# Sliding windows by DMA alone: the software ring's rows in 63 small DMAs over the run, let go by SyncE's

## The chip, the cores and the metric

One Trainium2 chip, one of its cores. The metric is the device time of one execution in microseconds (us), the median over runs of the same kernel. A core has 16 DMA engines, which move the data, and several instruction engines, which issue the DMAs. Three of them do so here: SyncE (SP in the profile), ScalarE (ACT) and GpSimd (POOL). Each has a ring of DMA work of its own on all 16 DMA engines. SP's is queue q1 and ACT's q10, both hardware_dynamic, and POOL's is q0, software_dynamic. I call q0 the software ring.

## What is computed

```python
batch, length, dim = (32, 4096, 256)      # float32
window_size, stride = 64, 32
n_windows = (length - window_size) // stride + 1        # 127
for i in range(n_windows):
    start = i * stride
    result[:, i] = x[:, start:start + window_size].copy()
```

It is a pure copy. A batch row of x has 128 blocks of 32 x 256 floats (32 KB each). Window w is blocks w and w + 1, 64 KB in a row, in x as in the output. So each block is written twice, but for the first and the last of a batch: 32 x 127 x 64 KB = 266.3 MB of output.

## The kernel before

The 32 batches are divided in two sets (L151 to L153).

**Staged** batches, 12 of them, go through SBUF on ACT's ring (class Staging). A load (L40) brings the 128 blocks of a batch, 4 MB, into one of six tiles xb; the stores (L49) then write it twice, once as the first half and once as the second half of the windows, in DMAs of 4 MB or 2 MB. Their pieces are 16 KB (IN and OUT, L9). `run` (L121) loads six batches, stores them, loads six more as their tiles come free, and stores those. The last two batches are stored by `store_pair` (L102), which waits once, near the end of the run, until four of its 2 MB stores have landed (semaphore `spilt`).

**Direct** batches, 20 of them, go from x to the output without SBUF. A DMA of SP (`windows`, L29, called by `blocks`, L166) takes one half (32 KB) of each of 16 windows: 512 KB in 16 pieces of 32 KB (DIRECT, L9). 16 x 7 = 112 of a batch's 127 windows go so, in 14 DMAs (`halves`, L174), 280 DMAs in all. 22 of these (`spoilt`, L175) lie next to a staged batch and come last, each after a wait for that batch's stores.

The other 15 windows of each direct batch, windows 48 to 62, are whole rows of 64 KB and go by POOL's ring (`remainder`, L170): one DMA of 15 rows for each of 19 batches; those of the last batch go in one DMA of 11 rows and four DMAs of two half rows. That makes 24 DMAs, 19.66 MB. `piece` is the largest run that one descriptor moves. It is 32 KB, and 16 KB for the 15 rows of the batches with index 0, 1, 2 and 6 and for the half rows.

All of this stands in one critical section (L178): ACT runs Staging, POOL issues its 24 DMAs one after the other without waiting and then drains (L189), and SP issues its 280. SP issues the first of them (L191), then waits for the semaphore `back` (L192), which the DMA of 15 rows of the batch with index 16 of 20 raises when it has landed, and then issues the rest (L193). At the end SP waits for all counts (L200).

The outermost count of an SP DMA's shape is 16 windows; of a POOL DMA's it is the number of rows.

Of the kernel before, what the change touches and what calls it, by code (L numbers as in the profile page):

```python
# [8 lines left out]
DIRECT, IN, OUT = 32768, 16384, 16384  # L9
# [124 lines left out]
@with_exitstack  # L134
def kernel(
    ctx: ExitStack,
    tc: tile.TileContext,
    x: bass.AP,
    window_size: bass.AP,
    stride: bass.AP,  # L140
    out: bass.AP,
):
    nc = tc.nc
    W, S = int(window_size), int(stride)
    B, L, D = x.shape
    n_win = (L - W) // S + 1
    assert out.shape == (B, n_win, W, D)
    c = Copier(x, out, B, L, D, W, S, n_win)


    staged = [1, 4, 7, 10, 13, 16, 19, 22, 24, 26, B - 3, B - 2]  # L151
    place = {b: g for g, b in enumerate(staged)}
    direct = [b for b in range(B) if b not in staged]  # L153
    pool = ctx.enter_context(tc.tile_pool(name="xb", bufs=1))
    st = Staging(c, tc, pool, x.dtype, staged, 6)
    ring_d, ring_s, ring_r = nc.sync, nc.scalar, nc.gpsimd
    done = tc.alloc_semaphore("done")
    rest = tc.alloc_semaphore("rest")
    back = tc.alloc_semaphore("back")
    total = {done: 0, rest: 0, back: 0}  # L160

    def count(dma, sem):
        dma.then_inc(sem, 16)
        total[sem] += 16

    def blocks(part):  # L166
        for b, w, half in part:
            count(c.windows(ring_d, b, w, 16, half), done)

    def remainder(i, b, w, n, half=None, piece=DIRECT):  # L170
        count(c.windows(ring_r, b, w, n, half, piece), back if i == len(direct) - 4 and n == 15 else rest)

    first, last = 48, B - 1
    halves = [(b, w + (15 if w >= first else 0), half) for b in direct for w in range(0, 112, 16) for half in (0, 1)]  # L174
    spoilt = {(b + d, 0 if d > 0 else c.nw - 16, 0 if d > 0 else 1): g for b, g in place.items() for d in (1, -1) if b + d in direct}  # L175
    halves = [h for h in halves if h not in spoilt]
    spoilt = sorted(spoilt, key=spoilt.get)
    with tc.tile_critical():  # L178
        st.run(ring_s)

        pairs = iter([(first + d, half) for d in (0, 2) for half in (0, 1)])
        for i, b in enumerate(direct[:-1]):
            if i in (12, 15, 17, 18):
                w, half = next(pairs)
                remainder(i, last, w, 2, half, DIRECT // 2)
            if i == len(direct) - 2:
                remainder(i, last, first + 4, 11)
            remainder(i, b, first, 15, piece=DIRECT // 2 if i in (0, 1, 2, 6) else DIRECT)
        ring_r.drain()  # L189

        blocks(halves[:1])  # L191
        ring_d.wait_ge(back, 16)  # L192
        blocks(halves[1:])  # L193
        for h in spoilt:
            b = h[0] + (-1 if h[1] == 0 else 1)
            st.wait_stored(ring_d, place[b])
            blocks([h])
        total[st.ended] = st.count[st.ended]
        for sem, n in total.items():
            ring_d.wait_ge(sem, n)  # L200
# [35 lines left out]
```

## Time and profile before

| what | value |
|---|---|
| three runs | 749.26, 749.43, 750.36 us; median 749.43 |
| the profiled execution | 747.93 us |
| its span, first to last instruction | 746.1 us |
| HBM read and written | 216.79 MB and 267.12 MB |
| SP's DMAs, 512 KB, issue to landing | 84.0 us (median) |
| POOL's 24 DMAs are issued | 1.51 to 15.06 us from the start |
| POOL's drain | 12.56 to 105.64 us |
| SP's second DMA is issued | 84.79 us |
| SP's last two DMAs are issued | 701.91 and 702.46 us |

There is no arithmetic, so the engines' busy shares say nothing. What is to be read is the DMA side. The row "DMA" of the profile's slices is the mean busy share of the 16 DMA engines in tenths, and the row "GB/s" is what they moved in each fortieth of the span (18.65 us). The section on queues counts packets, which are the single records of a DMA engine: a data piece, or the 4-byte write that raises a semaphore. The windows view gives, for a stretch of time, the share of the DMA engines and their GB/s as its last two numbers. A share can come out a little over 1 because records overlap by some ns and a record belongs to the stretch in which it starts. The trace also holds each record's own duration: their medians are 1213 ns for a piece of 32 KB (on q0 and q1 alike), 611 ns for one of 16 KB (on q0 and q10), and 9 ns for a semaphore write.

### The profile page before, as it was taken

Reading aid. Unit: us, or ns where it says so; the run is one execution under the profiler, and the core shown is the slowest. Engines: PE = TensorE matmul, PEld = TensorE weight load, DVE = VectorE, ACT = ScalarE, POOL = GpSimd, SP = SyncE. Lnnn points to the kernel's source line nnn. Section 1 sums busy time; section 2 is a strip of 40 time slices with the busy share of each in tenths; the row PEclk is TensorE's granted clock in tenths of the full one; section 3 lists DMA queues with packets and bytes.
Section 4 is the critical chain, followed back from the end, with each engine's and each line's share of the span. In section 5 each row is a group of like instructions: output and inputs, shape, how many; then the busy total and the mean of one; then the engine's idle time right before and its main releaser. Section 6 shows DMA issues by size and latency. Waiting matters only on the chain. (4 is left out here: it accounts for less than half of the span.)

```text
span 746.1 us, 413 instructions
## 1 busy us (share of the span) xinstructions
POOL 13.8 (2%) x28
## 2 busy tenths in 40 slices
POOL 7000000000000000000000000000000000000000
DMA  8999999999999999999999999999999999999997
GB/s 365 425 427 417 430 417 432 430 429 435 436 421 432 428 434 434 428 430 432 434 407 427 431 434 429 436 433 428 429 433 432 430 431 431 430 432 433 431 431 336
DMA packets 20306, 317.50 MB, mean 426 GB/s; under 512 B 5880, under 2 KB 5880, under 8 KB 5880
## 3 DMA queue, kind: packets, MB, share of 16 engines
q10 hardware_dynamic: 10064, 151.00, 47.6%
q1 hardware_dynamic: 8960, 146.82, 46.0%
q0 software_dynamic: 1280, 19.66, 6.2%
q14 instruction: 2, 0.02, 0.0%
HBM read 216.79 MB, written 267.12 MB: 649 GB/s over the span
## 5 line engine op out<-in xcount | busy, mean ns | idle before, releaser
L34 POOL DMA_DIRECT2D out_dram<-in_x_dram x24 | 13.6, 571 | 1.1 <-PEq L231 1.1
L217 POOL MEMSET const-float32-0.0<- 128x1 f32 x1 | 0.1, 98 | 0.2 <-issue 0.2
L217 POOL MEMSET const-bfloat16-1.0<- 128x1 bf16 x1 | 0.1, 101 | 0.0
L217 POOL MEMSET const-float32-1.0<- 128x1 f32 x1 | 0.1, 98 | 0.0
L217 POOL MEMSET const-uint8-127<- 128x1 uint8 x1 | 0.1, 98 | 0.0
## 6 DMA issues: line engine op xcount, KB each, us to landing
out_dram<-in_x_dram SPq DMA_DIRECT2D x280, 512.0 KB, 84.0
out_dram<-xb ACTq DMA_DIRECT2D x28, 2048.0 KB, 106.2
xb<-in_x_dram ACTq DMA_DIRECT2D x11, 4096.0 KB, 121.2
out_dram<-xb ACTq DMA_DIRECT2D x10, 4096.0 KB, 120.8
out_dram<-in_x_dram POOLq DMA_DIRECT2D x19, 960.0 KB, 44.1
xb<-in_x_dram ACTq DMA_DIRECT2D x4, 1024.0 KB, 13.9
out_dram<-in_x_dram POOLq DMA_DIRECT2D x1, 704.0 KB, 84.7
out_dram<-in_x_dram POOLq DMA_DIRECT2D x4, 64.0 KB, 69.2
```

The lines of the kernel that those rows point to most:

```text
L34: return q.dma_start(out=self.oap((b * self.nw + w0) * 2 + h, [[2 * blk, n], row]), in_=self.xap(b * self.nb + w0 + h, [[blk, n], row]), m ...
L217: nc = _bacc.Bacc("TRN2", target_bir_lowering=False, num_devices=1)
```

## The change

The wait on `back` is gone: SP issues its DMAs from the start. POOL's DMAs are made smaller. A list `drip` holds them, 15 rows as three DMAs of 5, the 11 rows as 6 and 5, and the four of two half rows as before: 57 + 2 + 4 = 63. POOL issues the first at once. Before each of the other 62 it waits for a semaphore of its own (`marks`), which one of SP's 258 DMAs raises when it has landed; these 62 are spread evenly over the 258 (the 5th, 9th, 13th and so on to the 254th). Of these 258 every fourth DMA (64) has pieces of 16 KB where it had 32 KB; the 22 spoilt ones keep 32 KB. The rows of the four batches that POOL moved in pieces of 16 KB have 32 KB now. The bytes, ACT's program and the set of SP's DMAs are the same.

```diff
-    back = tc.alloc_semaphore("back")
-    total = {done: 0, rest: 0, back: 0}
+    total = {done: 0, rest: 0}
 
     def count(dma, sem):
         dma.then_inc(sem, 16)
-        total[sem] += 16
-
-    def blocks(part):
+        if sem in total:
+            total[sem] += 16
+
+    def blocks(part, piece=DIRECT, sem=done):
         for b, w, half in part:
-            count(c.windows(ring_d, b, w, 16, half), done)
-
-    def remainder(i, b, w, n, half=None, piece=DIRECT):
-        count(c.windows(ring_r, b, w, n, half, piece), back if i == len(direct) - 4 and n == 15 else rest)
...
+    last, pairs = direct.pop(), iter([(d, half) for d in (0, 2) for half in (0, 1)])
+    drip = []
+
+    def odd(b, w, n, size):
+        drip.extend((b, first + w + k, min(size, n - k), None) for k in range(0, n, size))
+
+    for i, b in enumerate(direct):
+        if i in (12, 15, 17, 18):
+            w, half = next(pairs)
+            drip.append((last, first + w, 2, half))
+        if i == len(direct) - 1:
+            odd(last, 4, 11, 6)
+        odd(b, 0, 15, 5)
+    marks = [tc.alloc_semaphore(f"mark{i}") for i in range(len(drip) - 1)]
+    at = [len(halves) * (i + 1) // len(drip) for i in range(len(marks))]
+
     with tc.tile_critical():
         st.run(ring_s)
 
-        pairs = iter([(first + d, half) for d in (0, 2) for half in (0, 1)])
-        for i, b in enumerate(direct[:-1]):
-            if i in (12, 15, 17, 18):
-                w, half = next(pairs)
-                remainder(i, last, w, 2, half, DIRECT // 2)
-            if i == len(direct) - 2:
-                remainder(i, last, first + 4, 11)
-            remainder(i, b, first, 15, piece=DIRECT // 2 if i in (0, 1, 2, 6) else DIRECT)
+        for i, (b, w, n, half) in enumerate(drip):
+            if i:
+                ring_r.wait_ge(marks[i - 1], 16)
+            count(c.windows(ring_r, b, w, n, half, DIRECT if half is None else DIRECT // 2), rest)
         ring_r.drain()
 
-        blocks(halves[:1])
-        ring_d.wait_ge(back, 16)
-        blocks(halves[1:])
+        for i, h in enumerate(halves):
+            sem = marks[at.index(i)] if i in at else done
+            blocks([h], DIRECT if i % 4 != 2 else DIRECT // 2, sem)
         for h in spoilt:
             b = h[0] + (-1 if h[1] == 0 else 1)
             st.wait_stored(ring_d, place[b])
```

More of the change, by code (lines that the diff above doesn't have):

```diff
@@ L158 @@
     rest = tc.alloc_semaphore("rest")
-    back = tc.alloc_semaphore("back")
-    total = {done: 0, rest: 0, back: 0}
+    total = {done: 0, rest: 0}
     def count(dma, sem):
         dma.then_inc(sem, 16)
-        total[sem] += 16
-    def blocks(part):
+        if sem in total:
+            total[sem] += 16
+    def blocks(part, piece=DIRECT, sem=done):
         for b, w, half in part:
-            count(c.windows(ring_d, b, w, 16, half), done)
-    def remainder(i, b, w, n, half=None, piece=DIRECT):
-        count(c.windows(ring_r, b, w, n, half, piece), back if i == len(direct) - 4 and n == 15 else rest)
-    first, last = 48, B - 1
+            count(c.windows(ring_d, b, w, 16, half, piece), sem)
+    first = 48
     halves = [(b, w + (15 if w >= first else 0), half) for b in direct for w in range(0, 112, 16) for half in (0, 1)]
```

## The prediction

> **What bounds the kernel now.** I read the page's slices and queues first, then SP's waits, then the rate in stretches cut where the queues change.
>
> ```profile
> DMA  8999999999999999999999999999999999999997
> GB/s 365 425 427 417 430 417 432 430 429 435 436 421 432 428 434 434 428 430 432 434 407 427 431 434 429 436 433 428 429 433 432 430 431 431 430 432 433 431 431 336
> ...
> q10 hardware_dynamic: 10064, 151.00, 47.6%
> q1 hardware_dynamic: 8960, 146.82, 46.0%
> q0 software_dynamic: 1280, 19.66, 6.2%
> ```
>
> The 16 DMA engines are full from the first slice to the last, and the three queues' shares add up to 99.8% of the span. So the time is bytes over rate, plus a start and an end. The bytes don't change. A wait of a queue costs something only if the others leave DMA engines empty meanwhile.
>
> ```profile
> SPq L34 <- DMA out_dram<-in_x_dram: 83.2, 1, 83.2
> SPq L34 <- DMA out_dram<-xb: 43.4, 2, 39.9
> SPq L200 <- DMA out_dram<-xb: 40.5, 1, 40.5
> ```
>
> SP waits 83.2 us for `back`, later 39.9 us for the staged stores, and at last for the end. The windows view tells what the first of these costs:
>
> ```profile
> 20.00:84.00 64.00, 0.00 (x0) 1.00 1.01 425
> 84.00:100.00 16.00, 0.00 (x0) 1.00 1.00 427
> 100.00:104.00 4.00, 0.00 (x0) 1.00 1.05 389
> 104.00:370.00 266.00, 0.00 (x0) 1.00 1.01 431
> 370.00:382.00 12.00, 0.00 (x0) 1.00 1.00 392
> 382.00:702.00 320.00, 0.00 (x0) 1.00 1.01 431
> ```
>
> The last two numbers of a row are the DMA engines' share and GB/s. While SP waits (20 to 84), POOL's and ACT's queues fill the engines, at 425 against the 431 of SP and ACT later. With all three it is 427 (84 to 100), as the software ring empties 389 (100 to 104). The twelve us at 392 lie where ACT goes from stores to loads. How the queues share an engine is seen in the queues' packets from 105 to 740 us, without the software ring:
>
> ```profile
> q1 hardware_dynamic: 8706, 142.62, 52.5%
> q10 hardware_dynamic: 8693, 130.50, 48.1%
> ```
>
> The packets are equal (8706 to 8693) and the bytes are not: the queues take turns record by record, a semaphore write counting like a piece. From 20 to 80 us POOL and ACT stand at 787 to 775, the same rule.
>
> **The change part by part, in us of one execution.**
>
> *The wait on `back` removed: 0.* It is covered by POOL's and ACT's work at a share of 1.01. Without that cover it would cost up to 83.2.
>
> *SP and ACT from the start: 0.* With turns record by record, the queue with fewer records ends first. A DMA engine has for ACT 10064 / 16 = 629 records. For SP it has 560 before; 64 DMAs get one more each: 624. So the two still end within 5 records, some 5 x 0.6 = 3 us, of each other, and in that rest ACT alone fills the engines. Before, SP began late and from 84.79 us had 279 x 2 = 558 records left, ACT about as many. What hides a mismatch is the other queue's backlog: SP's DMAs land 84.0 us after issue. SP's 39.9 us wait for the staged stores is covered by that backlog, before as after. Without a backlog it would show whole; I see nothing that shortens the backlog by half.
>
> *Pieces: +0.4.* SP: 64 x 16 = 1024 pieces of 32 KB become 2048 of 16. POOL: 240 of 16 become 120 of 32. Net 904 fewer of 32 KB and 1808 more of 16. By the page a 16 KB piece with its share of semaphore writes takes 0.476 x 746.1 x 16 / 9216 = 0.617 us, a 32 KB piece with its write 0.460 x 746.1 x 16 / 4480 = 1.226. 1808 x 0.617 - 904 x 1.226 = 7.2 over 16 engines: +0.45 us. By the records' medians (611 and 1213 ns) it is 8.1 / 16 = +0.5. I take +0.45.
>
> *Semaphore writes: +0.5.* The software ring has 1280 packets, 728 of them data, so 552 / 24 = 23 small ones a DMA. 39 DMAs more make 897, at 9 ns in the records, over 16: +0.50. Lower bound: 5 a DMA in place of 23 gives 63 x 5 = 315, fewer than now, -0.13.
>
> *POOL's issues: 0.* 63 in place of 24, 571 ns each, 36 us in all on an engine that does nothing else, over a run of 746.
>
> *The 62 waits on POOL: 0.* Behind each stand POOL's later DMAs, its drain, and SP's last wait for `rest`. SP's 280 DMAs land over some 742 us, one each 2.65; a mark is every 4.1st, so POOL is let go about each 10.8 us, the last time at 254 x 2.65 = 673. A DMA of 5 rows is ten pieces. If five engines take two each, that is three turns of up to 1.2 + 1.2 + 0.6, some 9 us (estimate from the records' durations). The ring ends near 682, 60 us before the end. If POOL's DMAs landed as late as the 44.1 us of the page's row, it would be 717, still hidden.
>
> *Which engines five rows use: 0, bounds 0 and +2.5.* The trace doesn't name the engine of a record. Before, 15 rows can't have been the same for all 16 engines each time, and still the last 16 semaphore writes of SP's queue, one an engine, lie between 742.0 and 744.4 us, apart by one row (two pieces, 2.4 us). I take that the rows go round, and that the total is as even as before. One row too many on an engine is +2.5. The Trainium skill has such a rule ("DMA: Bandwidth & Descriptors", section "Why a DMA increments its semaphore by 16 and not by 1"): a software DMA whose outer count k isn't 16 goes to k engines in a row from a cursor that moves round. By it 296 rows give an engine 18 or 19, before and after; the even end agrees.
>
> *What the software ring costs beside others: 0, bounds -1.45 and +8.0.* Before, its phase loses 64 x 6 / 431 = 0.89 and 20 x 12 / 431 = 0.56 us (the mean of 84 to 104 is 419): 1.45. If that goes by its bytes, which are the same, nothing changes. If a thin ring costs nothing, it is -1.45. If it costs 6 GB/s for as long as it is in use, it is 680 x 6 / 431 = 9.5, less 1.45: +8.0. Nearest is the stretch where all three queues work, 427, and most of its 16 us show records at their medians, so I take 0.
>
> Sum: +0.45 + 0.50 = +0.9 (rounded down). The profiled execution's 747.93 becomes 748.8 and its span 747.0. The median lies 1.5 above that execution, so 749.43 + 0.9 = **750.3**. A measurement of this kernel can tell some 0.2%, 1.5 us: 747.93 to 750.93 is no change.
>
> **The rivals.**
>
> *Slower, the software ring taxes the whole run (0.22).* Each of its DMAs puts other engines out of step and takes rate from all three queues until about 680 us. For it: 425 and 419 in its phase against 431 after, and 389 as it empties. Against it: a share of that loss may come from its being mixed with loads and with the start. At 427 for 680 us the price is 680 x 4 / 431 = 6.3, less 1.45: 749.43 + 0.9 + 4.9 = 755.2; at 425 it is 758.3. It shows as slower from 429.7 down, since (431 - r) / 431 x 680 - 1.45 must exceed 0.6. The Trainium skill (the same page, "Latency and other measured facts") says that DMA engines 7 and 15 are usually slower, probably because all engines fetch the software ring's descriptors through their ports; this trace doesn't name engines, and their ends within 2.4 us speak against much of it.
>
> *Slower, an uneven end (0.14).* One engine gets a row more late, or ACT's last 6 MB come later: +2.5, 752.8. For it: one engine already ends 1 us behind the others (744.4 to 743.4). Against: 60 us without the ring at the end.
>
> *Faster (0.22).* The loss of the first 104 us goes (-1.45), and the drizzle breaks the step in which all engines meet ACT's change from stores to loads, 12 x 39 / 431 = 1.1: 749.43 + 0.9 - 2.5 = 747.8, and about 747 if the uneven end of 1 us goes too. For it: 600 us of SP and ACT show records at their medians, so the loss belongs to the ring and the changes. Against: that change has nothing of the ring in it now.
>
> *It doesn't do what it says (0.02).* All 63 DMAs on the same five engines: those would have 57 rows of 2.45 us each, 140 where 46 is the mean, some 845 us. The even end before speaks against it.
>
> **How the numbers follow.** The forecast has 0.40, with 749.0 to 751.0 as its own range: 0.36 within 0.2%, a little beyond on the slow side. The uneven end gives 0.02 to no change, the faster rival 0.02. So faster 0.20, same 0.40, slower 0.40. The range reaches from 747.4, inside the faster rival, to 755.5, past the tax at 427 GB/s; the tax at 425, the last case and the gains under 747.4 are left out, under 2 in 10.
>
> **What would show it.** Queue q1 with 280 x 16 + 3456 + 2048 = 9984 packets and the software ring with about 2057 over all slices to 680 us; SP and ACT equal in packets, both ending within 3 us; 430 to 431 GB/s in the middle. A middle of 427 or less means the tax; a last slice below 320 the uneven end; a first hundred us at 431 with no dip at ACT's change the faster rival. The forecast is wrong if the share of the DMA engines anywhere in the middle falls below 0.98.

## The result, and the profile after

The changed kernel takes 752.19 us (median of six runs, 751.32 to 753.64) beside 749.64 for the kernel before (749.26 to 750.5): a ratio of 1.0035, 95% interval 1.0021 to 1.0049. So it is 2.55 us slower here. In two later comparisons, on chips 7 and 12, the same two kernels stand at 1.0009 and 1.0005, with intervals that hold 1; the kernel before takes 746.2 to 746.7 us there and on chip 5, some 3 us less than here. Which chip this first comparison ran on is not on record.

The profiled execution took 751.59 us, its span is 749.8 against 746.1. The slices and the queues of the changed kernel's page (per queue: packets, MB, share of the 16 engines):

```profile
DMA  8999999999999999999999999999999999999997
GB/s 360 424 432 419 432 426 435 426 434 432 425 421 427 427 424 438 416 429 434 429 405 428 434 426 432 425 426 427 426 432 426 425 431 427 436 422 432 425 432 335
...
q10 hardware_dynamic: 10064, 151.00, 47.5%
q1 hardware_dynamic: 9984, 146.82, 46.1%
q0 software_dynamic: 3024, 19.67, 6.3%
```

The DMA engines are as full as before from end to end, yet more slices of the middle lie between 421 and 428 than before, where most stood at 428 to 435. Queue q1 has the 9984 packets that the change was worked out to give it; the software ring has 3024, not 2057. The windows view of the changed kernel, cut as the one before (POOL's busy time and instructions, granted clock, DMA share, GB/s):

```profile
20.00:84.00 64.00, 3.49 (x6) 1.00 1.01 426
84.00:104.00 20.00, 0.58 (x1) 1.00 1.01 430
104.00:370.00 266.00, 13.97 (x24) 1.00 1.01 428
370.00:382.00 12.00, 0.87 (x2) 1.00 1.02 410
382.00:680.00 298.00, 15.93 (x28) 1.00 1.01 428
```

The first hundred us gain a little (426 and 430 where it was 425 and 419). The 410 at ACT's change from stores to loads, where it was 392, is mostly the choice of the window, because the dip lies some us later now: from 360 to 396 us it is 420 where it was 418. The long middle loses: 428 against 431 over 564 us is 564 x 3 / 431 = 3.9 us. The gains give back 64 x 1 / 431 + 20 x 11 / 431 + 36 x 2 / 431 = 0.8.

The records tell of what kind the loss is. I call **excess** the sum, over all records of the three queues, of what each takes beyond the median of its kind (1213, 611 and 9 ns), per DMA engine. Over the run the records' medians add up to 740.4 us before and 742.0 after, and the excess is 4.3 us before and 6.8 after. Together that is 4.1 us more; neighbouring records overlap by some 3.4 ns each, which takes 0.6 off for the 2768 additional records. That leaves 3.5 of the 3.7 us by which the span grew. About 1.0 is records, 2.5 is excess. The medians differ by 2.55 only, because the profiled execution of the kernel before, 747.93, is shorter than all of its six runs; between median runs the excess would have grown by some 1.5 (an estimate: 2.55 less the 1.0 of the records). No wait leaves the DMA engines empty: SP's waits in the changed kernel are

```profile
SPq L34 <- DMA out_dram<-xb: 60.9, 4, 39.4
SPq L209 <- DMA out_dram<-xb: 37.2, 1, 37.2
```

and from 20 to 702 us the engines' share stays at 1.00 or more.

### The profile page after: what moved, and what is told of

Read it like the earlier page. It is cut to its first block, busy times and chain, and to the rows that moved or that the text cites. A ratio compares the mean times of both kernels' runs of the same rounds, so it can differ in the third digit from the quotient of the medians.

```text
span 749.8 us, 451 instructions
## 1 busy us (share of the span) xinstructions
POOL 36.9 (5%) x67
## 3 DMA queue, kind: packets, MB, share of 16 engines
q1 hardware_dynamic: 9984, 146.82, 46.1%
q0 software_dynamic: 3024, 19.67, 6.3%
## 4 chain that ended last, share of the span: by engine, by line
another core or an unknown queue 75%; DMA 6%; POOL 4%; issue 4%; SPq 2%; POOLq 0%
DMA out_dram<-in_x_dram 6%; POOL out_dram L34 4%; SPq L34 2%; POOLq L198 0%; SPq L240 0%; SPq L191 0%
## 5 line engine op out<-in xcount | busy, mean ns | idle before, releaser
L34 POOL DMA_DIRECT2D out_dram<-in_x_dram x63 | 36.7, 583 | 649.4 <-DMA out_dram<-in_x_dram 648.3
```

Of the source, the lines that this page charges most:

```text
L34: return q.dma_start(out=self.oap((b * self.nw + w0) * 2 + h, [[2 * blk, n], row]), in_=self.xap(b * self.nb + w0 + h, [[blk, n], row]), m ...
```

## The experiments

Twelve runs of ten kernels follow, on three chips, each beside the kernel before on its own chip. On chip 5 the changed kernel itself did not run. The last column is the excess of its profile.

| kernel | chip | median us | beside before | ratio, 95% | excess us |
|---|---|---|---|---|---|
| no_small_pieces | 5 | 753.15 | 746.70 | 1.0088, 1.0074 to 1.0102 | 8.0 |
| ring_at_start | 5 | 756.45 | 746.70 | 1.0132, 1.0119 to 1.0146 | 11.7 |
| drip_early | 5 | 752.95 | 746.70 | 1.0088, 1.0074 to 1.0102 | 7.3 |
| fifteen_rows | 5 | 750.62 | 746.70 | 1.0049, 1.0036 to 1.0061 | 6.3 |
| after_again | 7 | 746.82 | 746.24 | 1.0009, 0.9999 to 1.0018 | 2.1 |
| small_at_start | 7 | 766.98 | 746.24 | 1.0274, 1.0256 to 1.0291 | 22.5 |
| after_third | 12 | 746.57 | 746.37 | 1.0005, 0.9996 to 1.0014 | 2.1 |
| fifteen_again | 12 | 749.90 | 746.37 | 1.0045, 1.0031 to 1.0058 | 5.6 |
| more_small_pieces | 12 | 756.83 (one run) | 746.37 | | 11.6 |
| long_dmas | 12 | 767.57 | 746.37 | 1.0285, 1.0271 to 1.0299 | 20.7 |

Two more, even_ring and even_at_start (chip 7), leave part of the output out and are told of by their rates alone.

### Is it the wait, the pieces or the small DMAs?

**ring_at_start** is the change without its small DMAs: no wait, a quarter of SP's DMAs in 16 KB pieces, the ring's 24 DMAs at the start.

```diff
-        blocks(halves[:1])
-        ring_d.wait_ge(back, 16)
-        blocks(halves[1:])
+        for i, h in enumerate(halves):
+            blocks([h], DIRECT if i % 4 != 2 else DIRECT // 2)
```

> The kernel before without the wait for the software ring and with every fourth DMA of SP in pieces of 16 KB: the change without its 63 small DMAs. All three queues work from the start and the software ring empties after some 120 to 130 us. If the small DMAs over the whole run are the cause of the 2.5 us, this is near the kernel before, 749.6 + 0.5 for the pieces, 750.1, with an excess near 4.3 us and a middle at 430 to 431 GB/s. If the wait or the pieces are the cause, it is near 752.

It is 9.75 us slower than the kernel before, more than either case of the expectation. Its windows:

```profile
20.00:84.00 64.00, 0.00 (x0) 1.00 1.00 395
84.00:140.00 56.00, 0.00 (x0) 1.00 1.00 399
160.00:680.00 520.00, 0.00 (x0) 1.00 1.01 431
```

and its queues from 20 to 84 us (packets, MB, share of the 16 engines):

```profile
q0 software_dynamic: 534, 9.60, 37.1%
q10 hardware_dynamic: 531, 7.91, 32.9%
q1 hardware_dynamic: 533, 7.73, 30.3%
```

Three queues take turns exactly, the engines' share is 1.00, and yet only 395 GB/s go through; without the ring the same pieces go at 431. So the small pieces slow nothing by themselves: the loss lies in the time when three queues are backlogged, 8% of it. The ring ends at 151 us, and 64 x 36 / 431 + 67 x 32 / 431 = 10.3 us, less the 1.45 that its phase cost before and with the 0.5 of the pieces, comes near the 9.75. That is what the wait on `back` had kept apart.

**even_at_start** and **even_ring** ask whether uneven DMAs are the reason. Both leave the 19.66 MB of odd rows out of the output and move 37 of SP's DMAs of 16 pieces, one for each DMA engine, to the software ring; one issues them at the start, the other lets them go one by one.

```diff
+    drip = halves[3::7]
+    halves = [h for h in halves if h not in drip]
...
-            count(c.windows(ring_r, b, w, n, half, DIRECT if half is None else DIRECT // 2), rest)
+            count(c.windows(ring_r, b, w, 16, half), rest)
```

> The same 37 even DMAs on the software ring, all issued at the start, SP and ACT from the start too; the odd rows are left out. In ring_at_start, with uneven DMAs of 15 rows, 20 to 84 us went at about 398 GB/s with an excess of 8% of the time. If three queues at once are the cause, this shows the same 395 to 405 GB/s while the ring is in use; if uneven DMAs are, it shows 428 or more.

> The changed kernel with the odd rows left out (19.66 MB, some 45 us less) and 37 of SP's DMAs of 16 pieces moved to the software ring, let go one by one over the run. Each gives every DMA engine one piece, so nothing is put out of step. If being out of step is the cause, the middle runs at 430 to 431 GB/s with an excess under 0.3% of the time; if the third queue is the cause, the excess stays near 0.8% as in the changed kernel and the rate near 428.

even_at_start:

```profile
20.00:84.00 64.00, 0.00 (x0) 1.00 1.00 395
84.00:130.00 46.00, 0.00 (x0) 1.00 1.00 394
```

even_ring:

```profile
20.00:84.00 64.00, 1.53 (x4) 1.00 1.01 429
104.00:370.00 266.00, 7.81 (x16) 1.00 1.01 430
386.00:640.00 254.00, 6.34 (x13) 1.00 1.01 431
```

Even pieces, the same 395 when they stand in a queue; hardly a loss when they come one at a time. So the loss doesn't need uneven DMAs, and a third queue with little in it is nearly harmless. even_ring doesn't tell the two theories of its expectation apart on its own, since the changed kernel lost nothing on this chip either.

**after_again** and **after_third** are the changed kernel with no edit.

> The changed kernel unchanged, beside the kernel before on this chip, since the four runs so far stood beside a kernel before of 746.7 us in place of 749.6. If the difference is a property of the kernels and not of the chip, some 2.5 to 6 us over the kernel before; the profile's excess near 6.8.

> The changed kernel once more, beside the kernels below on one chip. So far it stood 0.35% over the kernel before with an excess of 6.8 us (the sum of the durations of the records over their medians) and in another call 0.09% with an excess of 2.1. The records alone give 0.13%. Expected between these; the excess tells which of the two this is.

Both lie below what was expected, with an excess of 2.1 us: after_again 0.58 us over the kernel before, where 2.5 to 6 had been expected, and after_third 0.20 (0.05%, where 0.09 to 0.35% had been). after_third:

```profile
20.00:84.00 64.00, 3.47 (x6) 1.00 1.01 430
104.00:370.00 266.00, 13.91 (x24) 1.00 1.01 431
382.00:680.00 298.00, 15.57 (x27) 1.00 1.01 431
```

The same program runs its middle at 431 here and at 428 in the first comparison. The additional excess there belongs to that comparison, perhaps to its chip or to where the arrays lay in its memory; no run tells which.

### How many pieces at a time

**fifteen_rows** lets the same rows go over the run in 24 DMAs of 15, and **fifteen_again** is the same kernel on the chip of after_third.

```diff
-            odd(last, 4, 11, 6)
-        odd(b, 0, 15, 5)
+            odd(last, 4, 11, 11)
+        odd(b, 0, 15, 15)
```

> The changed kernel with 15 rows to a DMA again (24 DMAs), still let go one by one over the whole run. Small records fall from 2416 to about 550, 1.0 us less an engine by 9 ns each, some 0.6 net of overlap. If a DMA of 5 rows hurts because 5 engines get work and 11 get none, 15 of 16 hurt less: excess near 5, time near 750. If the software ring taxes what runs beside it by its bytes or by its time in use, the excess stays near 6.8 and the time is some 751.5.

> The version with 15 rows to a DMA (24 DMAs over the run), which stood 0.49% over the kernel before where no run of the changed kernel stood beside it. If the size of the small DMAs matters, it differs here from the changed kernel by more than its records' 0.6 us; if not, it is 0.6 us shorter, and what it showed was that call's.

On the chip where the changed kernel takes 746.57 this takes 749.90: 3.3 us more, with 1872 records fewer. The windows of fifteen_again:

```profile
104.00:370.00 266.00, 5.18 (x9) 1.00 1.01 428
382.00:680.00 298.00, 6.31 (x11) 1.00 1.01 429
```

Of 104 to 370 us, the time in which a record of the ring is in flight is 43 us with an excess of 3.7%, and outside it the excess is 0.1%. In after_third it is 92 us with 0.1%. So the theory of uneven DMAs had it the wrong way round: DMAs of 15 rows slow what runs beside them, DMAs of five don't. The number of engines alone doesn't decide it: even_ring, one piece for each of 16 engines, has 0.3% in the same stretch, where 15 rows are two pieces for each. That the second piece makes the difference was not tested. In the first comparison the same count gives 101 us with 1.0%, and 0.4% outside, where the kernel before has 0.2%: there the slowing isn't bound to the time in which the ring moves. The two chips, 5 and 12, agree on this kernel (1.0049 and 1.0045), which lets what ran on chip 5 be read beside after_third with some care.

**drip_early** keeps the 63 DMAs and lets them go by SP's first 62 DMAs.

```diff
-    at = [len(halves) * (i + 1) // len(drip) for i in range(len(marks))]
+    at = list(range(len(marks)))
```

> The changed kernel with the same 63 DMAs of the software ring, let go by SP's first 62 DMAs one after the other in place of every fourth, so that the ring is in use for some 180 us in place of 697. The records are the same. If the cost goes by the time that the ring is in use, the excess falls from 6.8 toward 4.5 us and the time to about 750.0. If it goes by the number of uneven DMAs, the excess and the time stay near 6.8 and 752.2.

```profile
20.00:84.00 64.00, 11.59 (x20) 1.00 1.00 417
84.00:180.00 96.00, 17.33 (x30) 1.00 1.01 420
300.00:680.00 380.00, 0.00 (x0) 1.00 1.01 431
```

It is slow, 752.95, 6.25 us over the kernel before, though the ring is in use until 269 us (180 had been expected) in place of 697: the loss is packed into the time of use (417 and 420) and gone after it. A shorter time in use doesn't lower the price. The rate goes with how densely the ring's pieces come between the other two queues' pieces: 395 when it is always backlogged, 417 to 420 at this pace, 428 to 431 over the whole run.

**small_at_start** has the kernel before, with its wait, and the 63 small DMAs at the start.

```diff
-            remainder(i, b, first, 15, piece=DIRECT // 2 if i in (0, 1, 2, 6) else DIRECT)
+            for k in (0, 5, 10):
+                remainder(i, b, first + k, 5)
```

> The kernel before, with its wait, but with the software ring's rows in the 63 small DMAs, all issued at the start. Small records rise from 552 to about 2400, 1.0 us by 9 ns each, some 0.6 net. If small uneven DMAs by themselves slow the pieces, the excess rises from 4.3 toward 6.8 and the time by 3 us. If what slows the pieces is three queues at work at once, the wait still keeps SP out of the ring's phase: the excess stays near 4.3 and the time is 0.5 to 1 us over the kernel before.

20.7 us slower, which no theory had. SP's wait for `back` (SP's waits) and the windows show why:

```profile
SPq L34 <- DMA out_dram<-in_x_dram: 137.4, 1, 137.4
```

Then the windows:

```profile
20.00:84.00 64.00, 17.48 (x31) 1.00 1.01 429
90.00:140.00 50.00, 0.00 (x0) 1.00 1.00 402
690.00:750.00 60.00, 0.00 (x0) 1.00 1.00 335
```

With 5 rows to a DMA the ring moves some 6.5 KB in a turn where it moved 17, so it lasts until 175 us and SP waits 137.4 us in place of 83.2. ACT then ends early, and SP is alone from 690 to 764, at 335 GB/s; its pieces of 32 KB, 1213 ns beside ACT, take some 1570. That end makes up 74 x 96 / 431 = 16.5 us of the 20.7. The stretch from 90 to 140, POOL beside ACT's stores at 402, is told of below.

### The pieces, and the balance of the queues

**no_small_pieces** has all of SP's pieces at 32 KB.

```diff
-            blocks([h], DIRECT if i % 4 != 2 else DIRECT // 2, sem)
+            blocks([h], DIRECT, sem)
```

> The changed kernel with all of SP's pieces at 32 KB. By the records' medians (1024 pieces of 32 KB in place of 2048 of 16) it is 0.5 us shorter. If the small pieces are what slows the changed kernel beyond its records (the sum of record durations over their medians, the excess, is 6.8 us an engine in it and 4.3 before), the excess falls to about 4.3 and the time to some 749.5. If the software ring's small uneven DMAs are the cause, by being out of step or by being in use, the excess stays near 6.8 and the time near 751.7. SP has then 560 records an engine against ACT's 629, so SP ends early and ACT runs alone for some 40 us; if one queue alone cannot fill the engines, that end falls under 430 GB/s and the time is several us longer.

```profile
104.00:370.00 266.00, 14.55 (x25) 1.00 1.01 427
```

The small pieces are not the cause: without them the middle is still slow, the excess is 8.0, and 753.15 us is more than the 749.5 and the 751.7 of the expectation. By turns SP now moves 207 GB/s in the middle where it moved 196 to 198. ACT is left alone at the end for 12.5 us, not for 40, because SP, ahead of ACT, waits 119.7 us for the staged stores in place of 60.9. There ACT's pieces keep their 611 ns. **more_small_pieces** goes the other way, every second DMA.

```diff
-            blocks([h], DIRECT if i % 4 != 2 else DIRECT // 2, sem)
+            blocks([h], DIRECT if i % 2 else DIRECT // 2, sem)
```

> The changed kernel with every second DMA of SP in pieces of 16 KB in place of every fourth. By turns, record by record, SP then moves less in the middle (about 185 GB/s in place of 197) and HBM's read and write together fall from 655 to some 643 GB/s. If the excess of the middle comes from HBM at its limit, it falls to that of SP and ACT without the ring (0.1% of the time); if the software ring itself taxes, it stays as in the changed kernel of this call. SP's records are then more than ACT's by some 60, so SP is left alone at the end for 40 to 50 us at 330 GB/s, and the whole is some 8 to 12 us longer.

On this chip the changed kernel has no excess in the middle that could fall, so the first half of the question stays open. The second half came as expected, 10.3 us over after_third, by one run. Its window at the end:

```profile
702.00:745.00 43.00, 1.16 (x2) 1.00 1.01 342
```

SP is all but alone at the end (two DMAs of the ring fall there) and slow. With a quarter in small pieces SP and ACT end within 3 us of each other; with none and with a half they don't.

**long_dmas** was meant to be faster than both: 32 KB pieces on ACT's stores and five loads, SP's DMAs of 48 or 64 half windows.

```diff
-DIRECT, IN, OUT = 32768, 16384, 16384
+DIRECT, IN, OUT = 32768, 32768, 32768
...
-            max_dma_last_dim=IN,
+            max_dma_last_dim=IN if b % 2 else IN // 2,
...
+        for w, n in ((0, 48), (63, 64)):
+            for half in (0, 1):
```

> A version meant to be faster: the changed kernel with 32 KB pieces on ACT's stores and on five of its twelve loads, and SP's DMAs of 48 or 64 half windows, so that SP has about 382 records an engine and ACT about 397, equal turns again, and fewer semaphore writes. 4416 or so pieces of 32 KB in place of 16 KB pairs and 2850 fewer semaphore writes take some 3.5 to 4 us an engine less by the records' medians. Expected 0.3 to 0.5% under the changed kernel and 0.1 to 0.4% under the kernel before, unless larger pieces from SBUF are slower than 1213 ns or longer turns bring HBM to its limit more often.

It is 21.0 us slower than after_third. It has the fewer records, medians of 737.7 us an engine in place of 742.0, and 18.6 more of excess:

```profile
20.00:140.00 120.00, 6.95 (x12) 1.00 1.00 415
160.00:380.00 220.00, 11.01 (x19) 1.00 1.00 430
390.00:530.00 140.00, 7.51 (x13) 1.00 1.00 409
```

The records balance over the run as a whole (382 to 397 an engine; SP still ends 12 us ahead of ACT) but the bytes do not in each phase: while ACT loads, mostly in 16 KB pieces, SP's turns carry more, and the rate is 415 and 409; the stores go at 430. No version here beats the kernel before.

## Why the prediction was right, and where it wasn't

**The frame held.** The engines are full throughout, turns go record by record (from 105 to 680 us of the changed kernel q1 and q10 have 7754 and 7752 packets), the ends of SP and ACT lie within 3 us of each other (745.2 and 747.6), POOL's last DMA is let go at 686.0 where 673 was worked out, and q1 has the predicted packets. The 752.19 lies within the range, but outside the forecast's own 749.0 to 751.0: it is the room left for the rivals that holds it, and by the prediction's measure of 1.5 us it is a slower kernel in the first comparison.

**Pieces, +0.45: right.** Their medians come to +0.5 us.

**Semaphore writes, +0.50: too small by half.** The software ring has 2416 small records, not 63 x 23 = 1449. A DMA of 15 rows in 32 KB pieces accounts for 18, one of 5 rows for 38. The 1864 additional records of 9 ns are 1.05 us, 0.65 with their overlap. Pieces and small records together are +1.0 net of overlap, near the +0.9 of the sum; that they come so near is in part the overlap, which the sum left out.

**The software ring beside others, 0: this is the term that was off in the first comparison.** The excess rose by 2.5 us there between the profiles, some 1.5 between the medians, inside the bounds of -1.45 and +8.0, and the middle fell to 428, between the 430 of the forecast and the 427 of the tax. That is the slower rival in a small size: 427 had been priced at +4.9. On chips 7 and 12 the term is as forecast within the intervals: 0.6 and 0.2 us over the kernel before, where the records alone give 1.0. So the forecast of no change is right there and misses the first comparison by its excess. Why the first comparison shows it was not settled. A profile of the kernel before on chips 7 and 12, which would show its own excess, was not taken.

**Removing the wait, 0: right as a sum, wrong as an account of it.** I priced the wait by whether the engines had cover (a share of 1.01), and held that a wait costs only where engines stand empty. Full engines aren't all: ring_at_start has them full and loses 9.75 us, because the wait kept the third queue away. The zero holds only because the change also spreads the ring's DMAs, to which the prediction gave no part in it: that is luck. The nearest row that I took for three queues at once, 427 from 84 to 100 us, was no such row: SP had 95 packets there to ACT's 176, it had only begun. What buys the cost back is first the spreading over the run (15 rows a DMA: +0.5% where ring_at_start has +1.3%, both on chip 5) and then the small size (5 rows: +0.05% where 15 rows have +0.45%, both on chip 12). Small DMAs that aren't spread are dear (small_at_start +2.7%, drip_early +0.9%).

**A mismatch hidden by the other queue's backlog: half right.** ACT alone keeps its pieces at 611 ns. SP alone keeps the engines busy but not their rate (335 and 342 GB/s against 431), so a surplus of records on SP's side costs 21 to 22% of the time it lasts. In the changed kernel it is ACT that ends last, so the step did no harm.

**Uneven rows, 0 with +2.5: right.** The last 16 semaphore writes of SP's queue lie 2.6 us apart (742.6 to 745.2), where it was 2.4, so the total stayed about as even as before. The faster rival's mechanism shows in small (the first hundred us better), 0.7 us in the first profile, and was outweighed; ACT's change from stores to loads has its dip as before.

## What to carry to other kernels

A queue that waits may be waiting for a reason that the engines' busy share doesn't show: ask what rate the mix of queues goes at, and take it from a stretch where all of them are backlogged. Where queues take turns record by record, the size and number of records decide who ends first; match them over the run and in each of its phases, and let the queue that keeps the rate when it is alone be the last. Compare on more than one chip before a difference of 0.3% is put down to the kernel.

## What the runs showed of the hardware that was not expected

**A stream from HBM to HBM alone keeps the engines busy at a lower rate.** The queues of small_at_start from 700 to 750 us:

```profile
q1 hardware_dynamic: 1010, 16.55, 100.0%
```

16.55 MB in 50 us is 331 GB/s, read and written: 662 GB/s of HBM. In ring_at_start from 20 to 84 us the two direct queues count twice, ACT's once: (2 x (9.60 + 7.73) + 7.91) MB / 64 us = 665. SP and ACT together come to (2 x 142.62 + 130.50) / 635 = 655 in the kernel before, at 430 GB/s. That would fit a limit of HBM's read and write together near 660 GB/s, which SP and ACT just miss and a third, direct queue exceeds. It was argued from these sums, not tested by itself, and more such sums speak both ways: the slow stretches of no_small_pieces and drip_early come to 660 to 666, but SP at the end of more_small_pieces goes to 679 (705 to 745 us), and the slow middle of the first comparison to 650 to 654 only, less than the 656 to 658 of after_third, which isn't slow. The Trainium skill ("DMA: Bandwidth & Descriptors", "Issuing engines are not separate DMA queues") says that issuing from several engines only saves issue time. Here that isn't the whole of it: the third queue took the rate from 431 to 395.

**One stretch doesn't fit it.** small_at_start from 95 to 135 us, POOL's small DMAs beside ACT's stores:

```profile
q10 hardware_dynamic: 757, 11.19, 70.3%
q0 software_dynamic: 761, 4.92, 31.0%
```

That is 403 GB/s and (2 x 4.92 + 11.19) / 40 = 526 of HBM, far from 660, and the pieces are slow all the same (on average 1287 ns and 657). The same ring beside ACT's loads went at 429. The cause is open.

**A software DMA of few rows writes many small records.** The counts 552, 2416 and 544 (before, after, fifteen_rows) are met exactly by 16 a DMA and, for each engine without a row, one for each piece of a row: 16 + 2 x 11 = 38 for 5 rows, 16 + 2 = 18 for 15 rows. The trace doesn't name a record's engine, so where they are written is inferred from the counts. Each of them takes a turn (757 to 761 above), which is why the ring of small DMAs in small_at_start was so slow.

**A record is a turn, whatever its size.** An engine serves a 4-byte record and a 32 KB piece as one turn each, with three queues as with two: 534, 531 and 533 in ring_at_start.
